# Indexer scores of two heads on the two row halves of TensorE, in a hybrid attention and state-space layer

## The chip, the cores and the metric

The kernel runs on one core of one Trainium2 chip. The metric is the device time of one execution in microseconds (us), read from the chip; lower is better. The engines of the core are TensorE (PE in the profile, with PEld for its weight loads), VectorE (DVE), ScalarE (ACT), GpSimd (POOL) and SyncE (SP), whose queue issues the transfers between HBM and the chip's memory.

## What is computed

One layer of a streaming encoder: an input projection of x (1024 rows of 2048 columns), sparse attention on one half of its output, a Mamba-2 mixer on the other, an output projection and a LayerNorm. The change touches one part, the indexer of the attention. It gives each query a score for each key, and the 256 best keys are attended to:

```python
logits = jax.nn.relu(jnp.einsum('bqhd,bsd->bqhs', qib.astype(jnp.float32), k_idx32))
score = jnp.einsum('bqhs,bqh->bqs', logits, wb.astype(jnp.float32))
...
_, sel = lax.top_k(score, topk)
```

There are 16 indexer heads with 64 numbers each (`IDX_HEAD_DIM = 64`), all against one set of indexer keys of 64 numbers. Queries go in blocks of 128. Because the first 256 queries see at most 256 keys, only blocks 2 to 7 need scores.

## The kernel before

**Precision.** TensorE takes its inputs in fp32r, a shorter form of fp32. The kernel therefore splits each fp32 operand into a rounded part "hi" and a rest "lo", and builds a product as hi*hi + hi*lo + lo*hi. ScalarE makes hi (a copy that rounds), VectorE or GpSimd makes lo (a subtraction).

**Stages.** The sequence is cut into two halves h = 0 and 1 of 512 rows. The input projection (`emit_t`) runs through tiles of 128 output columns: one accumulation into a `pj` bank of PSUM is 8 blocks of 128 input columns times three matmuls of 128x512. The first tiles of half 1 (`misc`, which holds the indexer keys, and `qi` 0 to 7, the indexer queries, two heads to a tile) run plainly. After them, two groups of tiles follow with a scheme that needs fewer products but sums of quarter blocks of x, the "forms of x" (`t_xform`): four sets M2, M3, S1 and S4, loaded, added, and written back to HBM ahead of their use. The indexer tiles of half 0 stand in the opening of the first group.

**Order.** `Flow` plans the whole program while it is written out: a cost model (`Sim.cost`) keeps a clock for each engine, tasks are Python generators, and `pump` takes the first task in order of rank (lower is earlier) whose `Need` is met: engines not too far ahead, events there, and slots free. The rank of a task is the second argument of `fl.add`. Projection tiles are ranked 0, the score tasks `t_score` 0.5, the forms of x 1 (`form_tasks`). The engines then run their queues in the planned order and wait on semaphores.

**Slots.** PSUM has eight banks: four `pj`, three `a`, one `o`. The `a` banks serve the scores and all small matmuls; `o` serves attention outputs and the state-space outputs later on. `u` tiles are 128x512 buffers, 29 of them.

**The indexer.** `t_misc` makes the key operands of a half: `khh` holds the rounded keys twice, in rows 0 to 63 and again in rows 64 to 127; `k1` holds the rest of the keys in rows 0 to 63 and zeros below; `k2` holds zeros above and the rest of the keys in rows 64 to 127. `t_qi` applies the rotary embedding to a query tile `x` (head 2j in rows 0 to 63, head 2j+1 in rows 64 to 127) and makes two stationary operands: `a1`, with head 2j's hi on top and its lo below, and `a2`, with head 2j+1's lo on top and its hi below. Each score tile is then two matmuls that use all 128 rows:

```python
b = fl.new("a", [P, 512])
fl.mm(b[:, 0:m], lhs, khh[:, 0:m], stop=False)
fl.mm(b[:, 0:m], lhs, (k1, k2)[hh][:, 0:m], start=False)
fl.add(self.t_score(h, i, kh, m, head, b), 0.5, f"score{h}", fl.t)
```

The first gives (hi+lo) times hi, the second hi times lo. `t_score` takes the ReLU on ScalarE in place in the bank, and adds the weighted result to the score rows on VectorE, which frees the bank. There are 160 such tiles: 32 for half 0 (blocks 2 and 3, 8 tiles of two heads) and 128 for half 1 (blocks 4 to 7 against the keys of half 1, of which 128, 256, 384 and 512 are visible, and against all 512 keys of half 0).

When the last score of a half is there, `t_topk` finds the 256 best of each row, and the attention of that half can begin.

All instructions are recorded by one helper, line 312, so the profile tells them apart by their tiles: `a<-u,u` are the score matmuls in the first 340 us (later also matmuls of attention and of the mixer), `a<-a` the ReLU, `s<-a,wsc,s` and `u<-a,wsc,u` the weighted additions.

Of the kernel before, what the change touches and what calls it, by code (L numbers as in the profile page):

```python
# [10 lines left out]
R = mybir.dt.float32r  # L11
BF = mybir.dt.bfloat16
AF = mybir.ActivationFunctionType
ALU = mybir.AluOpType
# [3 lines left out]
HALF = 512  # L18
P = 128
# [99 lines left out]
def in_psum(x):  # L119
    return "PSUM" in str(x.space)  # L120
# [6 lines left out]
def kind_of(x):  # L127
    return str(x.dtype).split(".")[-1]


class Sim:
# [67 lines left out]
    def cost(self, eng, op, outs, ins, kw, n):  # L199

        if eng == "PE":
            n = ins[1].free_size()
            if op == "transpose":
                return 111.0, 290.0
            if kind_of(ins[1]) == "float32":
                if outs[0].partition_size() <= 64:
                    return 153.0, 300.0
                return 2 * max(n / 2.4 + 4, 100.0) if n > 8 else 226.0, max(n / 2.4, 57.0) + 330
            return n / 2.4 + 14.5 if n > 128 else max(n / 2.4 + 4, 80.0), n / 2.4 + 176
        if eng == "V":  # L210
            m = max(x.free_size() for x in [*outs, *ins])
            scalar = any(x.free_size() == 1 for x in ins) and n > 1
            if op in ("max", "match_replace"):
                t = (155 if op == "max" else 261) + 1.042 * m
            elif op == "bn_stats":
                t = 160 + 1.042 * m
            elif op == "stream_shuffle":
                t = 180 + 1.042 * n
            elif op == "tensor_tensor_scan":
                t = 200 + 2.084 * n  # L220
            elif op in ("tensor_scalar", "tensor_copy"):
                t = 145 + (1.042 if in_psum(ins[0]) or in_psum(outs[0]) else 0.64) * n + 45 * scalar
            elif op == "reciprocal":
                t = 145 + 5 * n
            elif op == "tensor_tensor_reduce":
                return 75 + 1.042 * n, 235 + 1.042 * n
            else:
                t = 145 + 1.042 * n + 60 * (op == "scalar_tensor_tensor" and scalar)
            return t - 80, t
        if eng == "A":  # L230
            t = (160 if in_psum(ins[0]) else 190) + 0.853 * n + 85 * (len(ins) > 1) + 100 * (len(ins) > 2)
            return (t - 15, t + 90) if len(outs) > 1 else (t - 97, t)
        if op == "memset":
            t = 90 + n
        elif op == "tensor_tensor":
            t = 180 + 2.16 * n if n > 8 else 600 + 120 * n
        else:
            t = 230 + 0.88 * n
        return t - 30, t
# [113 lines left out]
class Flow:  # L353
# [34 lines left out]
    def avail(self, tag):  # L388
        if tag == "us":
            return self.avail("u") + max(self.avail("s4") - self.spare, 0)  # L390
        if tag == "xs":
            return self.avail("xr") + max(self.avail("s4") - 1, 0)
        if tag == "ob":
            return self.avail("o") + max(self.avail("pj") - 2, 0)
        return sum(x[0] <= self.t + 300 for x in self.slots[tag])

    def new(self, tag, shape, dtype=F):

        if tag == "us":
            tag = "u" if self.avail("u") else "s4"  # L400
        if tag == "xs":
            tag = "xr" if self.avail("xr") else "s4"
        if tag == "ob":
            tag = "o" if self.avail("o") else "pj"
        free = self.slots[tag]
        assert free, ("no slot", tag)
        slot = min(free)
        free.remove(slot)
        self.n += 1
        home, i = slot[1]  # L410
        t = self.pool[home].tile(shape, dtype, name=f"{home}_{self.n}", tag=f"{home}{i}")
        self.where[t.tensor.name] = (tag, slot[1])
        return t
# [138 lines left out]
def f32(ap):  # L552
    return ap.bitcast(F)
# [14 lines left out]
class Layer:  # L568
# [199 lines left out]

    def form_tasks(self):
        for kp in range(4):  # L770
            self.fl.add(self.t_xform(kp), 1, f"xform{kp}")

    def request(self, n):
        for kp in range(4):
# [597 lines left out]

    def t_misc(self, h, j, ps):
        fl = self.fl
        yield Need("A", u=7)
        cos, sin = self.table("ri", h)
        mu = fl.new("u", [P, HALF])
        tmp = fl.new("u", [64, HALF])
        khh, k1, k2 = [fl.new("u", [P, HALF], R) for _ in range(3)]
        self.kk[h] = (khh, k1, k2)  # L1380
        fl.act(mu, ps)
        yield Need("PV", a=1)
        b = fl.new("a", [P, 4, P])
        for c in range(4):
            fl.tr(b[:, c], mu[:, c * P:(c + 1) * P])
        yield Need("VG")
        sd = getattr(self, f"sd{h}")
        wsc = sd["wsc"].rearrange("p (c n) -> p c n", c=4)
        raw = fl.new("sm", [P, 64]).rearrange("p (c n) -> p c n", c=4)
        fl.ts(wsc, b[:, :, 64:80], WSCALE, None, ALU.mult)  # L1390
        bias = self.hp[:, 0][:, None, :].to_broadcast([P, 4, 16])
        fl.tt("V", raw, b[:, :, 80:96], bias, ALU.add)
        fl.free(b)
        fl.signal(self.ev_w[h])
        fl.add(self.t_dt(h, raw), 1, f"dt{h}", fl.clk["V"])
        yield Need("V")
        yield from self.rope(mu[0:64], ps[0:64], tmp, cos[0:64], sin[0:64], self.SW8)
        fl.free(ps)
        yield Need("A")
        fl.act(khh[0:64], mu[0:64])  # L1400
        fl.act(khh[64:128], mu[0:64])
        yield Need("VG")
        self.nc.gpsimd.memset(f32(k1[64:128]), 0.0)
        self.nc.gpsimd.memset(f32(k2[0:64]), 0.0)
        self.sub("V", k1[0:64], mu[0:64], f32(khh[0:64]))
        self.sub("V", k2[64:128], mu[0:64], f32(khh[0:64]))
        fl.free(mu, tmp)
        fl.signal(self.ev_k[h])

# [51 lines left out]
    def t_qi(self, h, j, ps):  # L1461
        fl = self.fl
        n = 256 if h == 0 else 512
        s0 = 512 - n
        yield Need("A", u=4 + 2 * (("ri", h) not in self.tab), keep=3)
        cos, sin = self.table("ri", h)
        x, tmp = fl.new("u", [P, n]), fl.new("u", [P, n])
        a1, a2 = fl.new("u", [P, n], R), fl.new("u", [P, n], R)
        yield Need("V")
        yield from self.rope(x, ps[:, 0:n], tmp, cos[:, s0:], sin[:, s0:], self.SW8)  # L1470
        fl.free(ps)
        yield Need("A")
        fl.act(a1[0:64], x[0:64])
        fl.act(a2[64:128], x[64:128])
        yield Need("VG")
        self.sub("V", a1[64:128], x[0:64], f32(a1[0:64]))
        fl.two(a2[0:64], x[64:128], f32(a2[64:128]), ALU.subtract)
        fl.free(x, tmp)
        blocks = (2, 3) if h == 0 else (4, 5, 6, 7)
        if h not in self.score:  # L1480
            yield Need("", **({"u": 2} if h == 0 else {"s4": 4}))
            if h not in self.score:
                self.score[h] = {i: fl.new("u" if h == 0 else "s4", [P, 512 if h == 0 else 1024]) for i in blocks}
        if j == 7:
            fl.free(*self.tab["ri", h])
        first = True
        for kh in range(h, -1, -1):
            for hh, st in ((0, a1), (1, a2)):
                head = 2 * j + hh
                for bi, i in enumerate(blocks):  # L1490
                    q0 = i * P - h * HALF - s0
                    lhs = st[:, q0:q0 + P]
                    for kh in (kh,):
                        m = min((i + 1) * P - kh * HALF, HALF)
                        yield Need("PA", a=1, ev=(self.ev_k[h], self.ev_k[kh], self.ev_w[h]))
                        khh, k1, k2 = self.kk[kh]
                        b = fl.new("a", [P, 512])
                        fl.mm(b[:, 0:m], lhs, khh[:, 0:m], stop=False)
                        fl.mm(b[:, 0:m], lhs, (k1, k2)[hh][:, 0:m], start=False)
                        fl.add(self.t_score(h, i, kh, m, head, b), 0.5, f"score{h}", fl.t)  # L1500
        fl.free(a1, a2)

    def t_score(self, h, i, kh, m, head, r):
# [834 lines left out]
```

## Time and profile before

| what | us |
|---|---|
| median of three runs | 1693.85 |
| lowest and highest of them | 1691.37, 1695.41 |
| the profiled execution | 1696.48 |
| its span in the profile | 1694.7 |
| TensorE busy in the span | 1624.7 |
| VectorE busy in the span | 1329.2 |
| ScalarE busy in the span | 996.6 |

The span is the time from the first to the last instruction; about 1.8 us of the execution lie around it. Times in views are microseconds from the start of the span. Ends of matmuls are modelled and matmuls overlap, so the distance between starts, and not the listed duration, is what one matmul costs.

### The profile page before, as it was taken

How to read it: one execution, taken by the hardware profiler on the slowest of the kernel's cores; microseconds unless marked ns; L12 is line 12 of the kernel's file. 1: busy time of each engine (PE TensorE's matmuls, PEld its weight loads, DVE VectorE, ACT ScalarE, POOL GpSimd, SP SyncE). 2: the span in 40 equal slices, each digit the busy share in tenths (PEclk: the TensorE clock that was granted, in tenths of full speed). 3: DMA queues.
4: the chain of work that ended last, by engine and by line, in shares of the span. 5: the costliest groups of instructions: out<-in, count | busy, mean ns of one | idle time of the engine just before them, and what ended most of it. 6: DMA issues, size and time to landing. Idle time of an engine off the chain costs nothing.

```text
span 1694.7 us, 24018 instructions
## 1 busy us (share of the span) xinstructions
PE 1624.7 (96%) x7996; PEld 1341.5 (79%) x7996; DVE 1329.2 (78%) x2439; ACT 996.6 (59%) x1766; POOL 175.8 (10%) x205
## 2 busy tenths in 40 slices
PE   9999999998997999999999999999999999999997
PEld 7787788887875888778888888877787778788885
DVE  5889899987867886479776787866787676759998
ACT  4554666878777678784353556768657555442330
POOL 0000020001001000110210121112111011100110
PEclk9999999999998999999999999999999999999999
DMA  8288576889779866688746644665888998667754
GB/s 304 63 316 307 183 251 193 294 299 361 285 248 336 288 241 218 207 306 285 255 161 238 232 166 151 193 221 187 302 281 302 285 347 274 226 224 254 236 194 154
DMA packets 194149, 418.17 MB, mean 247 GB/s; under 512 B 19944, under 2 KB 55400, under 8 KB 194024
## 3 DMA queue, kind: packets, MB, share of 16 engines
q1 hardware_dynamic: 193592, 416.23, 72.1%
q8 instruction: 63, 1.03, 0.2%
q14 instruction: 62, 0.51, 0.1%
q10 hardware_dynamic: 432, 0.39, 0.1%
HBM read 310.77 MB, written 105.78 MB: 246 GB/s over the span
## 4 chain that ended last, share of the span: by engine, by line
PE 49%; DVE 22%; ACT 12%; DMA 10%; issue 6%; SPq 1%; POOL 1%; DVEq 0%; ACTq 0%; POOLq 0%
PE pj L312 36%; PE a L312 11%; DVE u L312 9%; ACT u L312 6%; DVE wl L312 4%; DVE s L312 4%; PE o L312 3%; DMA wr<-wt 3%; ACT wh L312 2%; DMA u<-u 2%; DVE xl L312 2%; ACT s L312 2%; DVE wr L312 1%; ACT L312 1%; DMA u<-wo 1%
## 5 line engine op out<-in xcount | busy, mean ns | idle before, releaser
L312 PE MATMUL pj<-xh,wh 128*128 128x512 f32 (+1 forms) x1496 | 584.0, 390 | 23.5 <-DVE u L312 12.9
L312 PE MATMUL pj<-xh,wl 128*128 128x512 f32 (+1 forms) x1496 | 573.0, 383 | 1.8 <-DVE wl L312 1.8
L312 PE MATMUL pj<-xl,wh 128*128 128x512 f32 (+1 forms) x1496 | 572.1, 382 | 0.0
L312 DVE TENSOR_TENSOR wl<-wr,wh 128x1024 fp32r<-128x1024 f32 (+2 forms) x235 | 280.2, 1196 | 162.8 <-ACT wh L312 159.7
L312 PEld LDWEIGHTS pj<-xh,wh 128*128 128x128 f32 x1496 | 283.3, 189 | 80.4 <-ACT u L312 16.6
L312 ACT ACTIVATE wh<-wr 128x1024 fp32r<-128x1024 f32 (+2 forms) x242 | 248.2, 1031 | 152.7 <-PE pj L312 122.3
L312 PEld LDWEIGHTS pj<-xh,wl 128*128 128x128 f32 x1496 | 282.7, 189 | 59.1 <-DVE wl L312 3.4
L312 PEld LDWEIGHTS pj<-xl,wh 128*128 128x128 f32 x1496 | 283.5, 190 | 50.3 <-DVE xl L312 0.4
L312 PE MATMUL a<-u,u 128*128 128x512 f32 (+3 forms) x744 | 174.1, 353 | 8.7 <-DVE s L312 4.9
L312 PEld LDWEIGHTS a<-u,u 128*128 128x128 f32 x744 | 122.7, 191 | 42.8 <-DVE s L312 18.8
L312 DVE TENSOR_TENSOR u<-u,u 128x512 f32<-128x512 f32 (+6 forms) x206 | 131.6, 648 | 18.7 <-DMA u<-wo 10.6
L312 ACT ACTIVATE u<-a 128x512 fp32r<-128x512 f32 (+4 forms) x115 | 53.7, 479 | 145.6 <-PE a L312 83.3
L312 ACT ACTIVATE u<-s,sm 128x768 bf16<-128x768 int16 (+7 forms) x132 | 129.5, 981 | 15.2 <-DVE sm L312 13.7
L312 PE MATMUL pj<-wh,xh 128*128 128x512 f32 x318 | 129.7, 408 | 1.2 <-ACT xh L312 1.0
L312 PE MATMUL pj<-wh,xl 128*128 128x512 f32 x318 | 124.9, 393 | 2.0 <-DVE xl L312 2.0
L312 PE MATMUL pj<-wl,xh 128*128 128x512 f32 x318 | 124.3, 391 | 0.0
L312 ACT ACTIVATE u<-u 128x512 f32<-128x512 f32 (+4 forms) x147 | 80.6, 558 | 62.1 <-DVE u L312 53.2
L312 ACT ACTIVATE a<-a 128x512 f32<-128x512 f32 (+3 forms) x160 | 76.1, 505 | 63.8 <-PE a L312 61.9
L312 DVE TENSOR_TENSOR wr<-wr,wr 128x1024 f32<-128x1024 f32 (+1 forms) x85 | 106.8, 1256 | 8.0 <-DMA wr<-wt 7.4
L312 DVE TENSOR_TENSOR u<-pj,u 128x512 f32<-128x512 f32 (+2 forms) x112 | 74.5, 666 | 38.9 <-PE pj L312 31.5
L312 POOL TENSOR_SCALAR s<-s,sm 128x640 f32<-128x640 f32 (+7 forms) x64 | 59.8, 947 | 295.9 <-DVE sm L312 208.8
L312 DVE SCALAR_TENSOR_TENSOR u<-cv,cw,u 128x512 f32<-128x512 f32 x96 | 72.1, 757 | 9.3 <-ACT u L312 4.3
(254 smaller groups left out, 2166.8 us busy)
## 6 DMA issues: line engine op xcount, KB each, us to landing
wr<-wt SPq DMA_DIRECT2D x187, 512.0 KB
u<-u SPq DMA_DIRECT2D x110, 256.0 KB
wr<-t SPq DMA_DIRECT2D x44, 512.0 KB
u<-wo SPq DMA_DIRECT2D x64, 256.0 KB
ts<-u SPq DMA_DIRECT2D x64, 256.0 KB
wr<-ts SPq DMA_DIRECT2D x32, 512.0 KB
s<-xt SPq DMA_DIRECT2D x24, 512.0 KB
t<-wr SPq DMA_DIRECT2D x22, 512.0 KB
```

Of the source, the lines that this page charges most:

```text
L312: f(*args, **kw)
```

## The change

Each score tile pair (two heads, one query block, one half of the keys) becomes one step. `a1` now holds hi of both heads, `a2` lo of both heads; `kl` holds the rest of the keys twice, in both row halves. A step makes six matmuls of 64 rows: for each of hi*hi, hi*lo and lo*hi one matmul on rows 0 to 63 for the first head and one on rows 64 to 127 for the second, into two banks. The banks come from `a` and `o` together. The planner prices a matmul of 64 rows at about half of one with 128 rows, `t_misc` needs one `u` tile fewer, and the forms of x are ranked 0.4, ahead of the score tasks.

```diff
@@ cost
+            if ins[0].partition_size() <= 64:
+                return n / 4.8 + 8, n / 2.4 + 176
             return n / 2.4 + 14.5 if n > 128 else max(n / 2.4 + 4, 80.0), n / 2.4 + 176
@@ avail
+        if tag == "ao":
+            return self.avail("o") + self.avail("a")
@@ new
+        if tag == "ao":
+            tag = "o" if self.avail("o") else "a"
@@ form_tasks
-            self.fl.add(self.t_xform(kp), 1, f"xform{kp}")
+            self.fl.add(self.t_xform(kp), 0.4, f"xform{kp}")
@@ t_misc
-        yield Need("A", u=7)
+        yield Need("A", u=6)
...
-        khh, k1, k2 = [fl.new("u", [P, HALF], R) for _ in range(3)]
-        self.kk[h] = (khh, k1, k2)
+        khh, kl = [fl.new("u", [P, HALF], R) for _ in range(2)]
+        self.kk[h] = (khh, kl)
...
-        yield Need("VG")
-        self.nc.gpsimd.memset(f32(k1[64:128]), 0.0)
-        self.nc.gpsimd.memset(f32(k2[0:64]), 0.0)
-        self.sub("V", k1[0:64], mu[0:64], f32(khh[0:64]))
-        self.sub("V", k2[64:128], mu[0:64], f32(khh[0:64]))
+        yield Need("V")
+        self.sub("V", kl[0:64], mu[0:64], f32(khh[0:64]))
+        self.sub("V", kl[64:128], mu[0:64], f32(khh[0:64]))
@@ t_qi
-        fl.act(a1[0:64], x[0:64])
-        fl.act(a2[64:128], x[64:128])
+        fl.act(a1, x)
         yield Need("VG")
-        self.sub("V", a1[64:128], x[0:64], f32(a1[0:64]))
-        fl.two(a2[0:64], x[64:128], f32(a2[64:128]), ALU.subtract)
+        fl.two(a2, x, f32(a1), ALU.subtract)
...
-            for hh, st in ((0, a1), (1, a2)):
-                head = 2 * j + hh
-                for bi, i in enumerate(blocks):
-                    q0 = i * P - h * HALF - s0
-                    lhs = st[:, q0:q0 + P]
-                    for kh in (kh,):
-                        m = min((i + 1) * P - kh * HALF, HALF)
-                        yield Need("PA", a=1, ev=(self.ev_k[h], self.ev_k[kh], self.ev_w[h]))
-                        khh, k1, k2 = self.kk[kh]
-                        b = fl.new("a", [P, 512])
-                        fl.mm(b[:, 0:m], lhs, khh[:, 0:m], stop=False)
-                        fl.mm(b[:, 0:m], lhs, (k1, k2)[hh][:, 0:m], start=False)
-                        fl.add(self.t_score(h, i, kh, m, head, b), 0.5, f"score{h}", fl.t)
+            for i in blocks:
+                q0 = i * P - h * HALF - s0
+                m = min((i + 1) * P - kh * HALF, HALF)
+                yield Need("PA", ao=2, ev=(self.ev_k[h], self.ev_k[kh], self.ev_w[h]))
+                khh, kl = self.kk[kh]
+                b = [fl.new("ao", [P, 512]) for _ in range(2)]
+                for n, (l, r) in enumerate(((a1, khh), (a1, kl), (a2, khh))):
+                    for hh in range(2):
+                        rows = slice(64 * hh, 64 * hh + 64)
+                        fl.mm(b[hh][:, 0:m], l[rows, q0:q0 + P], r[rows, 0:m], start=n == 0, stop=n == 2)
+                for hh in range(2):
+                    fl.add(self.t_score(h, i, kh, m, 2 * j + hh, b[hh]), 0.5, f"score{h}", fl.t)
```

## The prediction

> **What bounds the kernel now.** I read the page's busy times first, then its chain, then busy time by stage.
>
> ```profile
> PE 1624.7 (96%) x7996; PEld 1341.5 (79%) x7996; DVE 1329.2 (78%) x2439; ACT 996.6 (59%) x1766; POOL 175.8 (10%) x205
> PE 49%; DVE 22%; ACT 12%; DMA 10%; issue 6%; SPq 1%; POOL 1%; DVEq 0%; ACTq 0%; POOLq 0%
> 42.00:340.00 298.00, 288.29 (x1444) 236.28 (x1443) 269.56 (x457) 185.17 (x330) 24.88 (x22) 0.99 0.68 230
> 340.00:420.00 80.00, 77.02 (x336) 62.48 (x335) 63.94 (x142) 63.21 (x127) 7.57 (x6) 1.00 0.92 325
> 420.00:540.00 120.00, 101.84 (x427) 81.44 (x428) 89.32 (x213) 90.22 (x181) 3.76 (x4) 0.95 0.82 287
> ```
>
> The columns of the last three rows are the stretch, its length, the busy time of PE, PEld, DVE, ACT and POOL, the granted clock, the DMA share and GB/s. TensorE is the bound: it is busy 96% of the span and stands first in the chain. Where do the scores lie?
>
> ```profile
> L312 ACT ACTIVATE a<-a x160: 211/578/602, 50.0 to 337.8; 128x512 f32<-128x512 f32 x96, 128x384 f32<-128x384 f32 x32, 128x128 f32<-128x128 f32 x16, 128x256 f32<-128x256 f32 x16
> ```
>
> All 160 ReLUs run from 50 to 338 us, so the first stretch, 42 to 340, is the score stage. There PE is busy 288.3 of 298 us and DVE 269.6 (90%): a matmul saved there is time saved, with DVE close behind. The row also gives the sizes: 96 tiles of 512 keys, 32 of 384, 16 of 256 and 16 of 128. In pairs of heads these are 48, 16, 8 and 8, so the changed kernel makes 80 visits of six matmuls.
>
> **What the score matmuls cost.** PE's timeline, where x2 is one score tile:
>
> ```profile
> 121.39 0.39 PE L312 MATMUL pj<-xh,wl 128*128 128x512 f32 x1
> 121.61 0.33 PE L312 MATMUL a<-u,u 128*128 128x128 f32 x2
> 121.78 0.45 PE L312 MATMUL pj<-xh,wh 128*128 128x512 f32 x1
> 122.07 0.39 PE L312 MATMUL pj<-xl,wh 128*128 128x512 f32 x1
> 123.20 0.40 PE L312 MATMUL a<-u,u 128*128 128x256 f32 x2
> 123.44 0.40 PE L312 MATMUL pj<-xh,wh 128*128 128x512 f32 x1
> 124.83 0.51 PE L312 MATMUL a<-u,u 128*128 128x384 f32 x2
> 125.17 0.40 PE L312 MATMUL pj<-xh,wh 128*128 128x512 f32 x1
> 126.55 0.62 PE L312 MATMUL a<-u,u 128*128 128x512 f32 x2
> 127.00 0.39 PE L312 MATMUL pj<-xh,wh 128*128 128x512 f32 x1
> 1551.47 21.91 PE pj L312 x96
> ```
>
> Listed durations overlap, so I count from start to start. The last row is from the chain: 96 projection matmuls in 21.91 us, 0.228 each. Score tiles: 126.55 to 127.00 is 0.45, or 0.225 a matmul; 384 wide 0.17; 256 wide 0.12. At 128 wide it is 0.17, and the next matmul is late as well (0.29 to its successor, not 0.23): 0.23 for two, 0.115 each, twice what the widths above would give. There the weight load is the limit, some 0.11.
>
> **The six matmuls, if the halves overlap.** Two heads now cost four matmuls; then they cost three rounds of two.
> - 512 wide: 4 x 0.228 = 0.91 against 3 x 0.228 = 0.68, saving 0.228 on each of 48: 10.9 us.
> - Narrower visits depend on the weight loads, now six of 128 columns and not four. If the loads of the two halves run side by side, a quarter goes everywhere: 16 x 0.17 + 8 x 0.12 + 8 x 0.115 = 4.6, in all 15.5. If they queue at 0.11, a round takes at least 0.22: 384 wide 0.66 against 0.68 (16 x 0.02 = 0.3 gained), 256 wide 0.66 against 0.48 and 128 wide 0.66 against 0.46 (8 x 0.18 + 8 x 0.20 = 3.0 lost), in all 8.2.
>
> No row of before has two loads of different halves, so I take the middle, 12.
>
> **Going in and out of the half form.** Before has no matmul of 64 rows. It has two rows near it: a change of kind with all rows and columns (121.39 to 121.61 above: 0.22, no gap), and the mixer's matmuls on 64 columns:
>
> ```profile
> 911.88 1.05 PE L312 MATMUL a<-u,u 128*128 128x128 f32 x8
> 912.86 1.09 PE L312 MATMUL o<-s,u 128*64 128x128 f32 x16
> 913.88 0.50 PE L312 MATMUL pj<-xh,wh 128*128 128x512 f32 x1
> 914.22 0.39 PE L312 MATMUL pj<-xl,wh 128*128 128x512 f32 x1
> L312 PE MATMUL o<-s,u 128*64 128x128 f32 x160 | 11.6, 281 | 1.3 <-POOL s L312 1.3
> ```
>
> With 0.28 as the length of one, eight full matmuls start (1.05 - 0.28)/7 = 0.11 apart and sixteen of 64 columns (1.09 - 0.28)/15 = 0.054. The last full one starts at 912.65, the first narrow one 0.21 later (0.10 too late). The last narrow one starts at 913.67, the next full one 0.21 later (0.10 too late), and its successor 0.34 later (0.11 too late: its load wasn't made ahead). So a visit to the 64-column form loses 0.31 us. After a 512-wide matmul it can be more: a wait of 0.21 - 0.05 = 0.16 after the stream's end, then the load, 0.11, twice: 0.54. For the row halves I keep 0 to 0.54 a visit, 0 to 43 us in all. I take 0, going by the first row: here every load keeps its 128 columns and every output its 128 partitions of PSUM, while the gap in the trace comes with a load of other width. That is a choice, not a reading, and the break-even is low: 12/80 = 0.15 us a visit.
>
> The Trainium skill speaks against the change: TensorEngine Tiling, section Key Properties, says that changing the tiling mode drains TensorE. The trace agrees for columns (0.31 us); for rows no run here shows it yet, and by that rule the first rival below holds. TensorE: Matmul & The Clock Gate, Part 2, says that column tiling takes extra operand buses and row tiling none, which leans the other way.
>
> **Other parts.**
>
> ```profile
> L312 ACT ACTIVATE u<-u 64x512 fp32r<-64x512 f32 x20 | 12.6, 630 | 9.3 <-DVE u L312 9.0
> L312 ACT ACTIVATE u<-u 64x256 fp32r<-64x256 f32 x16 | 6.6, 413 | 7.3 <-DVE u L312 7.1
> L312 DVE TENSOR_TENSOR u<-u,u 64x512 fp32r<-64x512 f32 x19 | 13.4, 710 | 0.4
> L312 DVE TENSOR_TENSOR u<-u,u 64x256 fp32r<-64x256 f32 x15 | 6.6, 438 | 0.5
> PE a L312 <- DVE s L312: 4.9, 7, 2.9
> L312 PE MATMUL o<-s,u x162: 272/273/324, 696.3 to 1448.4; 128*64 128x128 f32 x160, 128*128 128x256 f32 x2
> ```
>
> - *Splits.* Each of 16 query tiles loses one ScalarE copy and one subtraction; 128 rows should take what 64 take, since the cost goes by the 256 or 512 elements of a row. ACT sheds 8 x 0.63 + 8 x 0.41 = 8.3 us, DVE (a little of it POOL) 8 x 0.71 + 8 x 0.44 = 9.2. PE's work covers them, so I cost them at nothing; they keep DVE at (269.6 - 9.2)/286, or 91%, as PE shortens the stage by 12. Without that cover DVE would be next.
> - *Banks.* A step now waits for two banks. Behind the waiting matmul stands PE's whole queue, the projection too, and behind that the ACT and DVE work on its banks. `o` gives a fourth bank, unused until 696 us (the last row). PE's waits for a bank that DVE's addition frees are 4.9 us (the wait row). That could grow as much as vanish; I take 1.5 off.
> - *Forms of x, memsets, the freed `u`.*
>
> ```profile
> L312 SPq DMA_DIRECT2D xfS<-s x8: 319/328/424, 93.0 to 246.6; - x8
> L312 SPq DMA_DIRECT2D xr<-xfM x8: 320/376/2156, 311.8 to 749.3; - x8
> 120.77 1.22 DVE L312 TENSOR_TENSOR s<-s,xr 128x1024 f32<-128x1024 f32 x1
> ```
>
> The last form is written at 247, the first is read at 312, so no one waits for them now: an earlier rank gains nothing directly. Its 16 sums of 1.2 us each now pass ahead of score additions on DVE, and its 32 transfers of 512 KB ahead on SP's queue. DMA has room (share 0.68) in this stage. Bounds: 4 us either way from the new order; value 0. The four memsets on POOL (busy 24.9 of 298) count nothing.
>
> **The sum.** Of 12 us at 338, not all arrives. From 340 to 540 DMA is at 0.92 and 0.82, and PE is idle 18 us of the last 120: transfers set part of the pace, and a PE that comes earlier partly waits longer. Since the stage before has DMA to spare, most of them move along; I keep 85%, 10.2. With 1.5 from banks: -11.7. Against the profiled execution, 1696.5 (span 1694.7 and 1.8 around it), that gives 1684.8. This execution was 2.6 above the median of 1693.85, so against the median I say 1682, with a range for this case of 1674 (15.5 + 4.9, nothing lost) to 1690 (8.2 x 0.85, less 4 for the order).
>
> **Rivals.**
> - *Each visit drains TensorE* (the other side). Place: the first and the last matmul of each of 80 visits. Price: 0.31, that is 25 us, less the 12 saved: +13, 1707; with 0.54 and queued loads 43 - 8 = +35, 1729. It decides from 0.15 a visit. For it: the gaps at 912.86 and 913.88. Against: they come with a change of column width, which isn't made. Chance 0.25.
> - *The halves don't overlap* (the change doesn't do what it says). Six matmuls in turn, two more: 48 x 0.456 + 16 x 0.34 + 8 x 0.24 + 8 x 0.23 = 31 us more, 1725. For it: no row shows two matmuls at once; the narrow ones at 0.054 are just 128 columns streamed, one after another. Against: nothing they use is shared, rows and banks both differ. Chance 0.07.
> - *The gain is given back* in the transfers of 340 to 540 and the new order: within 3 us, 1692. For it: the DMA pieces there and 18 us of PE idle. Against: PE idles just 25 us in the 1060 from 540 to 1600, so what passes 540 stays. Chance 0.16.
>
> ```profile
> 540.00:1600.00 1060.00, 1035.17 (x5265) 864.00 (x5265) 794.95 (x1457) 621.01 (x1078) 124.74 (x150) 0.99 0.72 245
> ```
>
> **How the numbers follow.** Forecast 0.52, drain 0.25, no overlap 0.07, given back 0.16. Faster by over 0.2% (3.4 us, about what a measurement here can tell from no change): 0.53 with a little of the last case; same 0.14; slower 0.33. The range goes from 1674 to 1716, into the drain case up to some 0.43 a visit with 12 saved; beyond lie the no-overlap case, the costliest drains, and a little below 1674: just under 0.2.
>
> **What would show it.** In PE's timeline, a 512-wide visit should take 0.7 us from its first matmul to the next `pj`; 0.9 to 1.2 with 0.2 gaps and late successors at both ends means draining; 1.35 without gaps, no overlap. A gap between rounds at 128 wide is queued loads. The ReLUs should end near 326, not 338. If they do and the end doesn't move, the stretch to 540 took it. The forecast falls if the gap at the row halves is over 0.15 us a visit.

## The result and the profile after

| | median us | lowest, highest | runs |
|---|---|---|---|
| before | 1693.74 | 1690.12, 1696.50 | 8 |
| after | 1704.09 | 1699.39, 1707.16 | 8 |

The change makes the kernel slower: the ratio is 1.0063, 95% interval 1.0045 to 1.0080, or 10 us. The forecast was 12 us the other way. In a later set of runs, on another chip, the changed kernel came out at 1.0084 (1.0068 to 1.0099).

The page of the changed kernel first, then its busy time by stage, in the columns used for before. Instructions that line 312 records in the kernel before stand at line 314 here.

```profile
span 1703.8 us, 24214 instructions
PE 1636.6 (96%) x8156; PEld 1333.7 (78%) x8156; DVE 1326.0 (78%) x2424; ACT 988.6 (58%) x1752; POOL 167.9 (10%) x200
```

```profile
42.00:340.00 298.00, 296.27 (x1647) 227.47 (x1646) 260.87 (x415) 167.28 (x297) 13.88 (x15) 1.00 0.63 222
340.00:420.00 80.00, 76.74 (x336) 62.33 (x335) 66.97 (x148) 56.52 (x114) 6.28 (x5) 1.00 0.93 340
420.00:540.00 120.00, 112.78 (x479) 91.44 (x478) 95.75 (x214) 97.60 (x193) 5.38 (x7) 0.96 0.80 285
540.00:1600.00 1060.00, 1021.67 (x5143) 849.14 (x5142) 781.61 (x1463) 627.89 (x1096) 129.97 (x152) 0.98 0.71 245
```

TensorE's busy time grew from 1624.7 to 1636.6 us, where 12 us less was expected. The score stage is fuller than before (296.3 of 298 us, not 288.3), so TensorE has more to do there, or takes longer. A full stage doesn't exclude lost time: a wide matmul is listed with 0.39 us and costs 0.23, so one that starts 0.1 us late leaves no idle time. Its timeline in a 512-wide visit shows which:

```profile
92.50 0.39 PE L314 MATMUL pj<-xh,wl 128*128 128x512 f32 x1
92.82 0.49 PE L314 MATMUL o<-u,u 64*128 64x512 f32 x1
92.82 0.49 PE L314 MATMUL a<-u,u 64*128 64x512 f32 x1
93.15 0.39 PE L314 MATMUL o<-u,u 64*128 64x512 f32 x1
93.15 0.39 PE L314 MATMUL a<-u,u 64*128 64x512 f32 x1
93.39 0.39 PE L314 MATMUL o<-u,u 64*128 64x512 f32 x1
93.39 0.39 PE L314 MATMUL a<-u,u 64*128 64x512 f32 x1
93.71 0.50 PE L314 MATMUL pj<-xh,wh 128*128 128x512 f32 x1
94.04 0.40 PE L314 MATMUL pj<-xl,wh 128*128 128x512 f32 x1
```

Read the starts. The two halves start together (92.82 and 92.82), so they overlap, as forecast. But the first round starts 0.32 after the last projection matmul and not 0.23 (0.09 lost); the second round starts 0.33 after the first (0.10 lost, and the first one is listed with 0.49, not 0.39: its load wasn't made ahead); the projection comes back 0.32 after the last round (0.09) and its own second matmul 0.33 later (0.10). From 92.50 to 94.04 is 1.54; less 2 x 0.228 for the projection matmuls at both ends, the visit costs 1.08 by these rounded starts. The 13 visits of this kind in the trace cost 1.09 or more, with a median of 1.10. Two tiles of four full matmuls cost 0.91, three rounds alone would cost 0.68. So entry and exit cost 0.41, nearly twice what the missing round saves.

A 128-wide visit, in the same view:

```profile
127.09 0.39 PE L314 MATMUL pj<-xh,wl 128*128 128x512 f32 x1
127.41 0.32 PE L314 MATMUL o<-u,u 64*128 64x128 f32 x1
127.41 0.32 PE L314 MATMUL a<-u,u 64*128 64x128 f32 x1
127.57 0.27 PE L314 MATMUL o<-u,u 64*128 64x128 f32 x1
127.58 0.27 PE L314 MATMUL a<-u,u 64*128 64x128 f32 x1
127.69 0.27 PE L314 MATMUL o<-u,u 64*128 64x128 f32 x1
127.69 0.27 PE L314 MATMUL a<-u,u 64*128 64x128 f32 x1
127.89 0.50 PE L314 MATMUL pj<-xh,wh 128*128 128x512 f32 x1
128.23 0.39 PE L314 MATMUL pj<-xl,wh 128*128 128x512 f32 x1
```

It costs 1.14 - 0.46 = 0.68, where the pair cost 0.45 or 0.46. The second and third rounds are 0.11 to 0.12 apart, the time of one load of 128 columns, though each round loads two sets of weights: the loads of the two halves go side by side. Read in the same way, 384 and 256 keys cost 0.92 and 0.77, against 0.70 and 0.47 before. No width wins.

Not all of the 80 visits pay: 14 follow straight on another one, which leaves 66 entries in the trace.

### The profile page after: what moved, and what is told of

It is laid out like the page before. It is cut to its first block, busy times and chain, and to the rows that moved or that the text cites. A ratio compares the mean times of both kernels' runs of the same rounds, so it can differ in the third digit from the quotient of the medians.

```text
span 1703.8 us, 24214 instructions
## 1 busy us (share of the span) xinstructions
PE 1636.6 (96%) x8156; PEld 1333.7 (78%) x8156; DVE 1326.0 (78%) x2424; ACT 988.6 (58%) x1752; POOL 167.9 (10%) x200
## 2 busy tenths in 40 slices
DMA packets 194149, 418.17 MB, mean 245 GB/s; under 512 B 19944, under 2 KB 55400, under 8 KB 194024
## 5 line engine op out<-in xcount | busy, mean ns | idle before, releaser
L314 PE MATMUL pj<-xh,wh 128*128 128x512 f32 (+1 forms) x1496 | 591.4, 395 | 12.9 <-DVE u L314 7.9
L314 PEld LDWEIGHTS pj<-xh,wh 128*128 128x128 f32 x1496 | 284.1, 190 | 85.1 <-issue 25.9
L314 PE MATMUL a<-u,u 64*128 64x512 f32 (+7 forms) x729 | 148.4, 360 | 5.1 <-DVE u L314 2.4
L314 ACT ACTIVATE u<-s,sm 128x896 bf16<-128x896 int16 (+7 forms) x132 | 129.6, 982 | 9.1 <-DVE sm L314 7.4
L314 PEld LDWEIGHTS a<-u,u 128*128 128x128 f32 (+1 forms) x729 | 102.8, 189 | 24.6 <-ACT u L314 4.0
L314 DVE TENSOR_TENSOR u<-u,u 128x512 f32<-128x512 f32 (+7 forms) x185 | 114.5, 631 | 9.4 <-ACT u L314 3.6
L314 ACT ACTIVATE u<-u 128x512 f32<-128x512 f32 (+3 forms) x129 | 71.0, 561 | 47.9 <-DVE u L314 42.9
L314 PE MATMUL o<-u,u 128*128 128x256 f32 (+4 forms) x417 | 82.6, 322 | 1.8 <-DVE s L314 1.1
```

The source lines that it names most:

```text
L314: f(*args, **kw)
```

## The experiments

The theory to test is that going in and out of the 64-row form costs some 0.41 us of TensorE each time, and that this makes the loss (A in the expectations). Its rivals: the new rank of the forms, the new order of the work, the wait for two banks, or a lower granted clock (0.980 in the profile after, 0.990 before). Edits named "in its order" keep the planner's prices and issue other matmuls, so the rest of the program keeps its order instruction for instruction.

### The forms of x alone

```diff
-            self.fl.add(self.t_xform(kp), 1, f"xform{kp}")
+            self.fl.add(self.t_xform(kp), 0.4, f"xform{kp}")
```

> The kernel before with one edit: the forms of x ranked 0.4 instead of 1. Theory A (the 10 us are the price of going in and out of the 64-row form, some 0.4 us a visit): the rank is not the cause, so the ratio to before is 1.000, within 0.998 to 1.002 (1690 to 1697 us). Theory B (the new order of the forms delays score additions and so the projection): this edit alone gives a good part of the loss, 1.003 or more (over 1699 us).

Measured: 1698.66 against 1689.98 us, ratio 1.0043 (1.0028 to 1.0058). That is the ratio of theory B, and against theory A. And the reverse, the changed kernel with the old rank:

> The changed kernel with the forms of x back at rank 1. Theory A (price of the visits): still slower than before by about as much as the changed kernel, ratio 1.004 to 1.009 (1701 to 1709 us). Theory B (rank of the forms): back to before or better, 1.000 or below.

Measured: 1707.06 us, ratio 1.0096 (1.0081 to 1.0111), a little above what A expected, and no better than the changed kernel. So the early rank costs in the old order and doesn't in the new one. The rank is not the cause in the changed kernel, but an order is worth more than I gave it; the runs on order below take that up.

### The price of entry by itself

The second matmul of a score tile has zeros in half of its rows. Leaving them out of the kernel before gives 64-row matmuls without any overlap to gain:

```diff
-                        fl.mm(b[:, 0:m], lhs, (k1, k2)[hh][:, 0:m], start=False)
+                        rows = slice(64 * hh, 64 * hh + 64)
+                        fl.mm(b[:, 0:m], lhs[rows], (k1, k2)[hh][rows, 0:m], start=False)
```

> The kernel before, where the second matmul of each score tile uses only the 64 rows that are not zero; same instructions otherwise, same order, same result. Nothing overlaps here, since each 64-row matmul stands alone behind a full one of its own bank, so it shows the price of going in and out by itself. Theory A: every one of 160 tiles goes in and out once at 0.3 to 0.45 us, so PE busy time and the end grow by 45 to 70 us (1738 to 1765 us, ratio 1.027 to 1.042). Rival (the row halves have no price of entry, and the changed kernel loses by its order or by waits for two banks): ratio 1.000, within 1691 to 1697 us.

Measured: 1735.30 us, ratio 1.0264 (1.0246 to 1.0282), 45 us more, just below the range of A and far from the rival. TensorE's busy time grew by 57 us, within A's range. The timeline of this run at a 512-wide tile:

```profile
122.44 0.39 PE L312 MATMUL pj<-xh,wl 128*128 128x512 f32 x1
122.67 0.82 PE L312 MATMUL a<-u,u 128*128 128x512 f32 x2
123.42 0.50 PE L312 MATMUL pj<-xh,wh 128*128 128x512 f32 x1
123.75 0.39 PE L312 MATMUL pj<-xl,wh 128*128 128x512 f32 x1
```

The x2 group holds the full matmul and the 64-row one. From 122.44 to 123.75 is 1.31, less 0.46 is 0.85 for a tile that took 0.45: again 0.40 for one entry and exit, here with a single 64-row matmul inside. The price is of the visit, not of each matmul.

The same edit on every second tile only (`rows = slice(64 * hh, 128)`, 80 entries in place of 160):

> As the run with the second matmul on its 64 rows, but only for the second head of each pair, so 80 of 160 tiles; same order as before. If the price goes by the number of visits: half of its 45 us, 1708 to 1716 us (ratio 1.011 to 1.016), and TensorE busy time up by some 29 us. If waits cover the first visits and only many of them show: under 1.008.

Measured: 1706.79 against 1690.97 us, ratio 1.0087 (1.0070 to 1.0104), 16 us; about a third of the 45, and between the two branches. TensorE's busy time rose to 1648.5 us with 80 entries and to 1682.2 with 160, that is by 24 and 57. Where a part of it goes is in the waits of weight loads in the score stage, here of before (42 to 340 us), of the run with 80 (42 to 354) and of the run with 160 (42 to 386), each to the end of its stage (what waited, for whom, us in total, times, longest):

```profile
PEld a L312 <- DVE s L312: 18.8, 37, 3.1
...
PEld pj L312 <- issue: 0.3, 2, 0.2
```

```profile
PEld a L312 <- issue: 25.6, 99, 0.4
PEld a L312 <- DVE s L312: 6.2, 17, 0.9
PEld pj L312 <- issue: 5.7, 26, 0.2
```

```profile
PEld a L312 <- issue: 50.4, 196, 0.4
PEld pj L312 <- issue: 12.4, 55, 0.3
...
PEld a L312 <- DVE s L312: 2.4, 8, 0.7
```

"Issue" is a wait that no semaphore explains; it is almost absent before and grows with the entries, to 31.3 and 62.8 us, 0.39 an entry in both: that is the price as the wait view shows it. The waits for score banks that VectorE frees (`DVE s`) shrink beside it, from 18.8 to 6.2 to 2.4. So the first entries fall partly into time in which TensorE would have waited for VectorE anyway: 31 us of price less 13 of such waits is near the 16 us at the end. For the next 80 there is little left to cover, 31 less 4, and they cost 29. The mean granted clock is 0.990 with 80 entries and 0.989 with 160, against 0.989 and 0.990 of the kernel before beside them, so the clock is not the cause.

### The change without its price

The changed kernel in its order, with three full matmuls in each visit:

```diff
-                        fl.mm(b[hh][:, 0:m], l[rows, q0:q0 + P], r[rows, 0:m], start=n == 0, stop=n == 2)
+                        fl.placed(fl.sim.run("PE", "matmul", [b[hh][:, 0:m]], [l[rows, q0:q0 + P], r[rows, 0:m]], {}))
+                for c, l, r, s, e in ((0, a1, khh, True, False), (0, a1, kl, False, True), (1, a2, khh, True, True)):
+                    fl.nc.tensor.engine.matmul(b[c][:, 0:m], l[:, q0:q0 + P], r[:, 0:m], start=s, stop=e, skip_group_check=False)
```

> The changed kernel in its very order, but each visit issues three matmuls of 128 rows (two into the first bank, one into the second) in place of six of 64 rows. It leaves out the separation of the two heads, so scores are sums over both heads; the work around it is unchanged. It shows what the change would have given had the entry and exit been free: 3 x 0.228 us a 512-wide visit. Theory A: faster than before by 8 to 15 us, 1679 to 1686 us, ratio 0.991 to 0.996. Rival (order, banks or transfers eat the gain whatever the matmuls cost): 1694 us or more, ratio 1.000 or above.

Measured: 1686.65 against 1689.98 us, ratio 0.9983 (0.9968 to 0.9997). It lies between the two: on the side of A, but 3 us, not 8 to 15. Its visit has no gaps (timeline of this run; line 1501 issues the score matmuls, and the first two are the x2 group):

```profile
89.31 0.39 PE L314 MATMUL pj<-xh,wl 128*128 128x512 f32 x1
89.54 0.62 PE L1501 MATMUL o<-u,u 128*128 128x512 f32 x2
90.00 0.39 PE L1501 MATMUL a<-u,u 128*128 128x512 f32 x1
90.22 0.39 PE L314 MATMUL pj<-xh,wh 128*128 128x512 f32 x1
90.45 0.39 PE L314 MATMUL pj<-xl,wh 128*128 128x512 f32 x1
```

From 89.31 to 90.45 is 1.14, less 0.46: 0.68, the price of three rounds as forecast. TensorE is busy 1608.3 us, 16 less than before. So each visit saves what it should, and most of it doesn't reach the end. Is that the fault of the new order? The kernel before in its own order, with one full matmul in place of two for every second head:

```diff
-                        fl.mm(b[:, 0:m], lhs, khh[:, 0:m], stop=False)
-                        fl.mm(b[:, 0:m], lhs, (k1, k2)[hh][:, 0:m], start=False)
+                        for k, r in enumerate((khh, (k1, k2)[hh])):
+                            fl.placed(fl.sim.run("PE", "matmul", [b[:, 0:m]], [lhs, r[:, 0:m]], {}))
+                            if k + hh < 2:
+                                fl.nc.tensor.engine.matmul(b[:, 0:m], lhs, r[:, 0:m], start=k == 0, stop=k + hh == 1, skip_group_check=False)
```

> The kernel before in its very order, but the second head of each pair gets one matmul of 128 rows in place of two, so a pair costs three full matmuls and not four, 15 us of TensorE less, with no visit to another form. It leaves out the hi times lo product of every second head. Together with the run of three full matmuls in the changed kernel's order (0.998 of before, with 16 us less of TensorE), it tells where the free saving goes. Theory A (the saving is worth most of its size, the new order of the changed kernel lost it): 1676 to 1681 us where before is 1690, ratio 0.992 to 0.995. Theory B (saved TensorE time is given back as later waits in any order): ratio 0.997 to 1.000.

Measured: 1685.64 against 1691.56 us, ratio 0.9953 (0.9935 to 0.9971), 6 us in the medians and 8 by the ratio of the 15 saved, between the two theories. TensorE is busy 1617.5 us, just 7 less than before. The waits of matmuls and of weight loads in its score stage, and its busy time there:

```profile
PE a L1501 <- DVE s L312: 7.7, 20, 1.2
```

```profile
PEld a L1501 <- DVE s L312: 25.9, 52, 1.4
```

```profile
42.00:340.00 298.00, 283.30 (x1389) 226.69 (x1388) 273.75 (x466) 190.39 (x339) 25.88 (x24) 1.00 0.68 236
```

Matmuls waited 4.9 us for VectorE's score additions before and wait 7.7 now, loads 18.8 and now 25.9. VectorE is busy 273.8 of 298 us in that stage, 92%: TensorE, made faster, runs into it.

### All of it side by side

> The changed kernel itself, on one chip with its two twins. Theory A (visits cost 0.41 us of TensorE each, some 27 us, of which waits that are there anyway cover a part): 0.006 to 0.009 above its twin with three full matmuls in the same order. Theory B (the order is what costs): within 0.003 of that twin.

> The changed kernel's order with three full matmuls a pair (the heads of a pair are not kept apart, as in the first run of this twin). Theory A: 0.995 to 1.000 of before. Theory B: 1.003 or more.

> The kernel before in its order with three full matmuls a pair (hi times lo of every second head left out, as in the first run of this twin). If about half of the 15 us saved arrives in before's own order, as in its first run: 0.994 to 0.997 of before. The distance to the twin in the changed order is then what order, banks and splits cost together, expected 0.002 to 0.004.

Measured on one chip, before at 1690.97 us:

| kernel | median us | ratio to before |
|---|---|---|
| before's order, three full matmuls | 1684.48 | 0.9965 (0.9953 to 0.9977) |
| changed order, three full matmuls | 1688.80 | 0.9979 (0.9968 to 0.9990) |
| changed kernel | 1706.18 | 1.0084 (1.0068 to 1.0099) |

So, in the medians of this chip: the saved round brings 6.5 us; new order, banks and splits together take back some 4 (the intervals overlap, so this part isn't settled); the entries cost 17.4 us, a ratio of 1.0105, between two programs of one order. That is more than the 0.006 to 0.009 of theory A and far from B. Both programs ran at a mean granted clock of 0.982, so the clock is no part of it. TensorE's busy time between those two is 1608.3 and 1636.6 us in the first pair of profiles, 28 us for 66 entries. Waits that were there anyway cover the rest: in the score stage of the first pair, matmuls wait 6.9 us for VectorE's score additions in the twin and 1.1 in the changed kernel, loads 13.6 and 6.2.

How much of this is there when the score stage ends? The ReLUs in `a` of the changed kernel, of its twin and of before's order with three full matmuls, in the first profiles (those in `o` end within 0.5 us of them):

```profile
L314 ACT ACTIVATE a<-a x113: 225/578/605, 50.6 to 335.1; 128x512 f32<-128x512 f32 x67, 128x384 f32<-128x384 f32 x23, 128x128 f32<-128x128 f32 x12, 128x256 f32<-128x256 f32 x11
L314 ACT ACTIVATE a<-a x113: 215/563/602, 50.3 to 322.1; 128x512 f32<-128x512 f32 x67, 128x384 f32<-128x384 f32 x23, 128x128 f32<-128x128 f32 x12, 128x256 f32<-128x256 f32 x11
L312 ACT ACTIVATE a<-a x160: 214/577/608, 50.7 to 332.9; 128x512 f32<-128x512 f32 x96, 128x384 f32<-128x384 f32 x32, 128x128 f32<-128x128 f32 x16, 128x256 f32<-128x256 f32 x16
```

Within one order, what the stage gains or loses is most of what the end shows. The price makes 13 us at the stage's end (322.1 to 335.1) and 17 at the end of the kernel. The free saving in before's order makes 5 us (337.8 to 332.9) and 6 at the end, so the rest of its 15 us is lost inside the stage, where VectorE is, and not in the transfers behind it. Between the orders it is not so: the twin ends its scores 11 us ahead of before's order (322.1 against 332.9) and, in the medians above, the kernel 4 us behind it. What the new order loses behind the score stage was not followed up.

### What an order is worth

One number of the planner changes. The matmuls are the same ones (x7996), though the planner also moves a few instructions from one engine to another, and with 12.5 ns it issues four more transfers (419.21 MB in all, not 418.17):

```diff
-            return n / 2.4 + 14.5 if n > 128 else max(n / 2.4 + 4, 80.0), n / 2.4 + 176
+            return n / 2.4 + 16.5 if n > 128 else max(n / 2.4 + 4, 80.0), n / 2.4 + 176
```

> The kernel before with one number of the planner changed, 16.5 in place of 14.5 ns on top of the columns of a wide matmul; every instruction is the same, only their order moves. It measures what a change of order alone can do. If order is worth little: ratio 0.998 to 1.002, and the 1.004 of the run with only the forms' rank is a property of the forms. If any new order moves the end by up to half a per cent: ratio off 1 by 0.003 or more, either way.

> The kernel before with 12.5 in place of 14.5 ns for a wide matmul in the planner; every instruction is the same. A fourth order for the kernel before (1.000, 1.004 with the forms' rank, 0.997 with 16.5). If orders scatter by half a per cent: 0.995 to 1.005, without a sign known ahead.

> The changed kernel with one number of the planner changed, 16.5 in place of 14.5 ns for a wide matmul, the same edit that moved the kernel before by -0.3%. With the orders tried so far (changed kernel 1.006, forms at the old rank 1.010, true price 1.015) it shows how far the loss depends on the order. Theory A (12 us more of TensorE time in any order, and an order worth half a per cent either way): ratio 1.002 to 1.015. Rival (the loss is bad luck of the orders drawn): ratio 1.000 or below.

And the changed kernel with the price of a 64-row matmul at `n / 4.8 + 76`:

> The changed kernel with one number of the planner changed: a matmul of 64 rows is priced at n/4.8 + 76 ns, which makes a visit cost what the trace of the changed kernel shows (1.10 us at 512 keys, 0.68 at 128). Theory A (the loss is TensorE time, 80 visits at some 0.41 us less what they save): a right price mends nothing, ratio 1.004 to 1.010. Theory B (the planner, thinking TensorE 0.4 us a visit ahead of where it is, put work in the wrong order): the loss goes, ratio 0.998 to 1.002.

| order | kernel before | changed kernel |
|---|---|---|
| as it is | 1 | 1.0063 (1.0045 to 1.0080), later 1.0084 (1.0068 to 1.0099) |
| other rank of the forms | 1.0043 (1.0028 to 1.0058) | 1.0096 (1.0081 to 1.0111) |
| 16.5 ns | 0.9968 (0.9956 to 0.9981) | 1.0056 (1.0040 to 1.0072) |
| 12.5 ns | 1.0109 (1.0092 to 1.0127) | not run |
| true price of a visit | not applicable | 1.0151 (1.0131 to 1.0170) |

With 16.5 ns the kernel before gets faster and with 12.5 ns slower than anyone would guess from two nanoseconds; both fall outside a span of 0.2%, one outside the half per cent that was expected. A planner that knows the true price of a visit does not mend the loss: 1.0151 is above both of the ranges expected, and it is one more order, so it doesn't tell a wrong price from a bad draw. Before's slower orders also ran at a lower mean granted clock: 0.990 and 0.990 for the two fastest, 0.986 with the other rank, 0.983 with 12.5 ns. Whether the clock made them slow, or fell because TensorE waited more, is not shown. So one pair of kernels, each with one order, can't show a change of half a per cent: the loss of 0.63% is within what orders do to the kernel before (0.9968 to 1.0109). Two things still hold. Four orders of the changed kernel all lie above 1.005, their mean is 1.009; the mean of the four of before is 1.003, which with four draws each points the same way and proves little. And the runs in one order, which don't have this scatter, show the price of the visits directly.

### Fewer visits

If the price is of the visit, two pairs a visit should pay it half as often. The edit takes two query blocks to a step, with `yield Need("PA", ao=4, ...)`, twelve 64-row matmuls and then four score tasks, priced for one entry.

> The changed kernel with two pairs of score tiles to a step, so four banks and twelve matmuls of 64 rows in a row, priced for one entry and exit. At most 40 visits in place of about 70. Theory A (price per visit of 0.41 us): TensorE busy time falls by about 12 us, and the time to about that of before, ratio 0.998 to 1.003. Rival (the price is of each 64-row matmul, not of the visit, or the wait for all four banks takes back what the visits save): ratio 1.005 or more.

Measured: 1699.46 against 1691.56 us, ratio 1.0044 (1.0026 to 1.0061). The trace has 40 entries. TensorE's busy time fell to 1627.9 us, 9 below the changed kernel; 26 entries at 0.41 would make 11. Since busy time also moves by 8 us among orders with the same matmuls (1624.7 before, 1632.6 with 16.5 ns), and this is another order, the fall agrees with the price but doesn't prove it. The time lies between the two branches: a little below the changed kernel's 1.0063, with overlapping intervals, and not at that of before. A second form lets a step also take idle projection banks:

```diff
         if tag == "ao":
-            return self.avail("o") + self.avail("a")
+            return self.avail("o") + self.avail("a") + max(self.avail("pj") - 2, 0)
...
-            tag = "o" if self.avail("o") else "a"
+            tag = "o" if self.avail("o") else "a" if self.avail("a") else "pj"
```

> As the run with two pairs a visit, but a step may also take idle projection banks, so it waits less for four free banks. Some 40 visits again. If the wait for banks is what kept two pairs a visit above before, the waits of TensorE in the score stage (5.8 us there) shrink and the ratio falls to 1.000 or below. If the remaining loss is the price of the visits and later waits, the ratio stays at 1.002 to 1.006.

Measured: 1729.56 us, ratio 1.0233 (1.0216 to 1.0250); a miss for both branches. Its page, span and TensorE:

```profile
span 1727.5 us, 24290 instructions
PE 1632.1 (94%) x8156; PEld 1336.1 (77%) x8156; DVE 1323.3 (77%) x2429; ACT 978.8 (57%) x1746; POOL 160.3 (9%) x195
```

TensorE is busy a little less than in the changed kernel (1632.1 us), but stands idle 95 us of the span, where it was 67. The waits of matmuls in the score stage did not shrink: by the wait view of 42 to 340 us they are 5.2 us with four banks and 6.8 here. The largest group of waits in the whole span is for ScalarE's operands of later projection matmuls (`PE pj` for `ACT xh`, 19.2 us, 5.2 in the changed kernel), 15.3 of it after 1560 us. So this run says little on banks; it is another order too, and the farthest off.

### Must the halves alternate?

The changed kernel in its order, with the loop over halves outside the loop over the three products, so the queue has three matmuls of rows 0 to 63 and then three of rows 64 to 127.

> The changed kernel in its order, but within a visit all three matmuls of rows 0 to 63 come first and then the three of rows 64 to 127. Same entries and exits, same instructions. If the halves overlap only when neighbours in the queue alternate, two of three rounds lose their overlap: a 512-wide visit grows from 1.10 to about 1.5 us, TensorE busy time by 20 us or more, and the time to 1716 to 1728 us (ratio 1.015 to 1.022). If TensorE can run a half ahead past the other half's queue, nothing changes: ratio 1.004 to 1.009.

Measured: 1706.71 against 1690.99 us, ratio 1.0093 (1.0077 to 1.0110), with TensorE busy 1637.6 us (1636.6 in the changed kernel). Overlap did not go. The timeline of this run, where the three `o` matmuls stand ahead of the three `a` matmuls in the program:

```profile
102.81 0.39 PE L314 MATMUL pj<-xh,wl 128*128 128x512 f32 x1
103.13 0.49 PE L1503 MATMUL o<-u,u 64*128 64x512 f32 x1
103.14 0.49 PE L1503 MATMUL a<-u,u 64*128 64x512 f32 x1
103.46 0.39 PE L1503 MATMUL o<-u,u 64*128 64x512 f32 x1
103.47 0.39 PE L1503 MATMUL a<-u,u 64*128 64x512 f32 x1
103.70 0.39 PE L1503 MATMUL o<-u,u 64*128 64x512 f32 x1
103.71 0.39 PE L1503 MATMUL a<-u,u 64*128 64x512 f32 x1
104.02 0.50 PE L314 MATMUL pj<-xh,wh 128*128 128x512 f32 x1
104.36 0.39 PE L314 MATMUL pj<-xl,wh 128*128 128x512 f32 x1
```

The fourth matmul that the program issues starts 0.01 us after the first. TensorE takes a half's matmuls past those of the other half, and the visit costs what it did.

## Why the prediction was wrong

- **Size and place of the score matmuls: right.** 80 visits, and full matmuls of the forecast sizes; a visit of three full rounds measured 0.68 us.
- **Overlap of the halves: right, and better than taken.** The halves start together; their loads go side by side (rounds 0.11 apart at 128 keys), so the upper bound of 15.5 us was the right saving, not the middle of 12.
- **Going in and out: this step failed.** "I take 0, going by the first row": of the two rows near the unknown I took the one that promised nothing, because the loads keep their 128 columns. Measured: 0.41 us at 512 keys, 0.34 to 0.41 at the others, in the changed kernel, and 0.40 at 512 in a run that has the visits and nothing else. With the order held, the entries cost 17.4 us at the end. The gaps have the look of the row that I set aside: a late start at entry and exit, and a late successor at each. Had its 0.31 been taken for the 80 visits, as the first rival did, the forecast would have been 1707. The break-even was 0.15 us as I put it, and 0.19 with the 15.5 us that the overlap does save; the known row lay above both, and that should have settled the choice. The Trainium skill, TensorEngine Tiling, section Key Properties, says that changing the tiling mode drains TensorE. The trace agrees for rows too, with 0.41 us for a visit; what it shows are late starts and late loads, not the draining itself.
- **How much of the saving arrives: too high.** I kept 85% of 12 us, for later transfers' sake. In before's own order 6 to 8 of 15 us arrived, and the loss came earlier than I looked for it: VectorE's score additions free the banks, and the waits for them grew (matmuls 4.9 to 7.7 us, loads 18.8 to 25.9). The last ReLU came 5 us earlier, not 15, so the transfers behind the stage were not what took the rest. I named VectorE as next, and costed it at nothing. Even with free visits, the forecast of -11.7 would have been missed at -2 to -3.
- **Splits: as forecast for ScalarE, without effect.** ScalarE's busy time fell by 8.0 us (996.6 to 988.6), VectorE's by 3.2 and not 9.2.
- **The order: far too narrow.** I gave 4 us either way. Orders moved the kernel before from -0.3% to +1.1%, some -5 to +18 us.
- **The rivals.** The draining rival was the right one. That its 13 us at a price of 0.31 came close to the 10 measured is luck: the price is higher, 66 entries pay it and not 80, waits for VectorE cover a part of the price as of the saving, and the order adds some 4. "The halves don't overlap" fell. "Given back" had a part of the amount and not the place: half of the saving goes to VectorE inside the score stage, not to the transfers of 340 to 540.

## What to carry to other kernels

Before packing half-height matmuls into a stream of full ones, count the changes of form: here each visit costs some 0.4 us of TensorE, nearly two 512-wide matmuls, while overlap saves one for each pair. So TensorE breaks even only at about two 512-wide pairs a visit (0.41 against 2 x 0.23), and here two pairs a visit still left 1.0044. When an unknown has two near rows that give opposite signs, set the break-even first and let the dearer row decide unless something excludes it. Where a planner orders the work, compare edits in one fixed order, because a new order can move the time by more than the edit does.

## What the runs showed of the hardware

- Two matmuls of 64 rows on the two row halves, into two banks, start within 0.01 us of each other and both run at nearly the full rate (0.24 us a round at 512 columns, 0.23 for one full matmul), and their weight loads go side by side (a round of two at 128 columns takes 0.11 us).
- They need not be neighbours in the queue: three of one half and then three of the other overlap as well (the fourth that was issued starts 0.01 us after the first).
- A change between 64-row and full matmuls costs about 0.2 us each way at 512 columns: 0.09 of late start, and 0.10 at the matmul after it, which fits a load that wasn't made ahead.
